# A state space stage laid out anew: half height blocks, three real products for a complex one, sums on the matrix engine

## The chip, the cores and the metric

One core of a Trainium2 chip runs the whole program in one launch. The metric is the device time in microseconds (us), median of three runs. TensorE (PE) multiplies matrices and transposes through an identity; VectorE (DVE) and GpSimd (POOL) do elementwise work; ScalarE (ACT) does activations and copies; SyncE (SP) issues most DMAs. Products accumulate in PSUM, which the other engines read.

## The reference, cut to what matters

Two model blocks on 256 tokens of width 2048: a diagonal state space mixer, two feed forward layers and an attention, then two layers that mix retention, attention and a recurrence. The change concerns the first stage alone:

```python
def s5_mixer(u, a_re, a_im, log_dt, b_re, b_im, c_re, c_im, d_skip, w_glu):
    lam_re, lam_im, dt = jnp.minimum(a_re, -1e-4), a_im, jnp.exp(log_dt)[:, None]
    mag, ang = jnp.exp(lam_re * dt), lam_im * dt
    lb_re, lb_im = mag * jnp.cos(ang), mag * jnp.sin(ang)          # lambda, [128 groups, 64 states]
    den = lam_re * lam_re + lam_im * lam_im
    nr, ni = lb_re - 1.0, lb_im
    coef_re = (nr * lam_re + ni * lam_im) / den
    coef_im = (ni * lam_re - nr * lam_im) / den
    bb_re = coef_re[..., None] * br - coef_im[..., None] * bi      # B bar, [g, p, 16]
    bb_im = coef_re[..., None] * bi + coef_im[..., None] * br
    ...                        # per group: s_t = lambda s_(t-1) + B bar u_t, from zero
    y = einsum('blgp,ghp->blgh', st_re, cr) - einsum('blgp,ghp->blgh', st_im, ci)
    g = jax.nn.gelu(y + d_skip * u)
    val, gate = jnp.split(g @ w_glu, 2, axis=-1)                   # the gated unit
    return val * jax.nn.sigmoid(gate)
```

Here u is the normed input in 128 groups of 16 channels; each group has 64 complex states.

## The kernel before, in words

`s5` (lines 257 to 743) does all up to the gelu; `glu` multiplies by `w_glu`. Tokens stand in 64 chunks of 4, groups are g = 64 gh + g'. V holds B bar times powers of lambda (a chunk's tokens into the state), W holds C times powers of lambda (state into the tokens), kd the blocks C lambda^d B within a chunk.

- Parameters: one group per partition. `exp_col`, sines and powers run on VectorE, squares of x for the norm on ScalarE. `regroup` orders x by group into M; `u_turn` transposes 64 blocks of 64x128; `u_scale` multiplies by the norm's scale on VectorE into U.
- `v_build` makes 8 blocks of 128x1024 by `cmul` (two products and a sum), 5 on VectorE and 3 on GpSimd. `w_build` makes 6 (3 and 3), `b_build` 2 on GpSimd.
- `turn` transposes four 128x128 blocks into a PSUM tile `psm`; `scatter` writes each tile by four ScalarE copies of 64x256 into `pad`, [128, gh, g', re/im, 64], where the rows of the other gh are zeros. GpSimd zeroes one quarter at the start and a DMA copies it to the other.
- `v_apply`: V x U for the states' inputs, over all 128 rows, in both column halves; ScalarE copies into S, [128, chunk, re/im, g'].
- kd: B bar x W in four column tiles (`psm<-pad,M`), four times: a ScalarE copy to `kd`, a GpSimd add of D, four DMAs to `kp` in DRAM and four back into M (lines 643 and 646).
- The scan (`step`, lines 651 to 673) on VectorE: four operations of 128x64 for each of 64 chunks, in two halves of the groups, the second 18 chunks behind.
- `own` adds U x M for all eight pairs of k-tiles, then `states` adds S x W; gelu on ScalarE, transposed and split in hi and lo (`split`), then the products of `glu`.

Every engine handle is wrapped by `InOrder`: ScalarE and GpSimd keep the order of the code from the start, VectorE and TensorE from the bar at line 396 on. All instructions of the stage carry line 230, that of the wrapper, so the profile tells them apart by their tiles. Tile x is also the store of the raw B and C. Behind the stage a steady loop of three products per weight tile runs (lines 65 to 67): load `wraw`, cast `whi` on ScalarE, subtraction `wlo` on VectorE.

Of the kernel before, what the change touches and what calls it, by code (L numbers as in the profile page):

```python
# [18 lines left out]
D = 2048  # L19
# [9 lines left out]
def load_unit(k, W, r0, nk, c0, cw):  # L29
    """k-tiles r0/128.. of W, split in two float32r parts whose sum is the float32 weight."""  # L30
# [83 lines left out]
def split_transposed(k, src, dst, kts, gain=None):  # L114
    """src(t, i): [128 tokens, 128] AP; dst hi/lo [128, k-tile, 256]; kts: k-tiles to fill."""
# [95 lines left out]
class InOrder:  # L211
    """an engine; after bar() instructions stay behind the last one, with strict each behind the one before"""
# [24 lines left out]
def exp_col(k, pool, x):  # L237
    """exp of [128, 1] to float32 rounding: 2**n times a polynomial of the rest"""
    nc = k.nc
    n = pool.tile([128, 1], F32, name="ec_n")  # L240
    p = pool.tile([128, 1], F32, name="ec_p")
    ni = pool.tile([128, 1], I32, name="ec_i")
# [14 lines left out]
def s5(k):  # L257
    """gelu of the state space mixer's output, transposed: hi/lo [128, k-tile, 256].

    Groups g = 64 gh + g'. Tokens go in 64 chunks of 4. The state times lambda, before each chunk:  # L260
    G' = lambda**4 G + sum_j lambda**(4-j) B u_j; y_l = C lambda**l G + sum_(j<=l) C lambda**(l-j) B u_j.
    """
# [36 lines left out]
    nc.sync.dma_start(dt, I["ssm_log_dt"][0].rearrange("(g o) -> g o", o=1))  # L299
    nc.sync.dma_start(ai, I["ssm_a_im"][0])  # L300
    nc.sync.dma_start(ar, I["ssm_a_re"][0])
    nc.sync.dma_start(gain, I["mix_norm"][0].rearrange("(g h) -> g h", h=16))
    for j in range(4):
        nc.sync.dma_start(xs[:, j, :], xr[:, j, :])
    for r, n in enumerate(("re", "im")):
        nc.sync.dma_start(braw[:, r], I["ssm_b_" + n][0])
    nc.sync.dma_start(pad[0:64, 1], pad[64:128, 0])
    nc.sync.dma_start(dsk, I["ssm_d"][0].rearrange("(g h) -> g h", h=16))
    for r, n in enumerate(("re", "im")):
        nc.sync.dma_start(craw[:, r], I["ssm_c_" + n][0])  # L310
# [3 lines left out]
    M = sU.tile([128, 2, 64, 64], F32, name="M")  # L314
    mflat = M.rearrange("p a b c -> p (a b c)")
    xn = mflat[0:64].rearrange("p (g a j h) -> p g a j h", a=2, j=4, h=16)
    junk = U[0:64].rearrange("p a b -> p (a b)")

    def regroup(j):
        o, i = xn[:, :, :, j, :], xs[:, j, :].rearrange("p (a g h) -> p g a h", a=2, h=16)  # L320
        if j == 3:
            nc.scalar.copy(o, i)
            return
        if j == 1:
            nc.gpsimd.tensor_copy(o, i)
            return
        nc.vector.bar()
        nc.vector.tensor_copy(o, i)
        nc.vector.bar()

    def square(j):
        nc.scalar.activation(junk[:, 0:D], xs[:, j, :], AF.Square, accum_out=ss[:, j:j + 1])

    regroup(1)
    for r in range(2):
        nc.gpsimd.tensor_tensor(
            braw[:, r], braw[:, r], gain.unsqueeze(1).to_broadcast([128, 64, 16]), ALU.mult
        )

    # parameters, groups on the partitions; pw[:, i] = lambda ** (4 - i)  # L340
    dtv = exp_col(ko, sB, dt)
    lr, th, sn, cs, em, nr, den, w0, tq, ang, cre = (
        sB.tile([128, 64], F32, name="p_" + n)
        for n in ("lr", "th", "sn", "cs", "em", "nr", "den", "w0", "tq", "ang", "cre")
    )
    mag, cim = th, ang
    nc.vector.tensor_scalar(lr, ar, -1e-4, None, ALU.min)
    cmul(den, tq, lr, lr, ai, ai, 1)
    nc.vector.reciprocal(den, den)
    nc.vector.tensor_scalar(th, lr, dtv, 0.5, ALU.mult, ALU.mult)  # L350
    nc.scalar.activation(th, th, AF.Tanh)
    nc.vector.tensor_scalar(ang, ai, dtv, None, ALU.mult)
    reduce_angle(ko, sB, ang, 64, wide=False)
    regroup(0)
    nc.vector.tensor_scalar(w0, ang, 0.5, None, ALU.mult)
    sincos(ko, sB, ang, 64, sn, cs)
    nc.scalar.activation(w0, w0, AF.Sin)
    nc.vector.tensor_scalar(em, th, -1.0, 1.0, ALU.mult, ALU.add)
# [3 lines left out]
    square(0)  # L362
    square(1)
    regroup(3)
    square(2)
    square(3)
# [9 lines left out]
    regroup(2)  # L376
# [8 lines left out]
    pc = sB.tile([128, 2, 4, 64], F32, name="pc")  # L385
    vpool = sB.tile([128, 2, 16, 64], F32, name="bb")
    t4 = vpool[:, 0, 0:4]
# [4 lines left out]
    cmul(pc[:, 0], t4, pw[:, :, 0], b1(cre), pw[:, :, 1], b1(cim), -1)  # L392
    cmul(pc[:, 1], t4, pw[:, :, 0], b1(cim), pw[:, :, 1], b1(cre), 1)
# [4 lines left out]
    def u_turn(g0, pool, nm):  # L398
        pt = pool.tile([128, 8, 64], F32, name=nm)
        for i in range(8):  # L400
            nc.tensor.transpose(pt[:, i, :], xn[:, g0 + i].rearrange("p a c d -> p (a c d)"), ident[:64, :64])
        return pt

    upt = [u_turn(8 * i, *((k.psg, "psg") if i < 4 else (k.psm, "psm"))) for i in range(6)]
    R = sA.tile([128, 64], F32, name="R")

    def rstd():
        rs = sA.tile([64, 4], F32, name="rs")
        nc.scalar.activation(rs, ss, AF.Sqrt, scale=1.0 / D, bias=k.eps[:64])
        nc.vector.reciprocal(rs, rs)  # L410
        rx = sA.tile([64, 2, 4, 16], F32, name="rx")
        nc.vector.tensor_copy(rx, rs.unsqueeze(1).unsqueeze(3).to_broadcast([64, 2, 4, 16]))
        pt = k.psm.tile([128, 64], F32, name="psm")
        nc.tensor.matmul(pt, rx.rearrange("p a c d -> p (a c d)"), ident[:64, :64], start=True, stop=True)
        nc.scalar.copy(R, pt)

    def u_scale(i):
        nc.vector.tensor_tensor(
            U[:, 8 * i:8 * i + 8, :], upt[i], R.unsqueeze(1).to_broadcast([128, 8, 64]), ALU.mult
        )  # L420
# [20 lines left out]

    def v_build(ri, b, on_pool=False, between=None):
        p0 = 16 * b
        if on_pool:
            eng = nc.gpsimd
# [112 lines left out]
    for i in range(4):  # L558
        u_scale(i)
# [921 lines left out]
```

## Time and profile before

| | |
|---|---|
| median of 3 runs | 3307.14 us (3305.91 to 3307.64) |
| profiled execution, span | 3304.2 us |
| PE, DVE, ACT, POOL busy | 97%, 59%, 49%, 3% of the span |
| instructions PE, DVE, ACT, POOL | 16691, 2983, 2151, 51 |
| TensorE's share of the chain that ended last | 90% |

The span is that of one profiled execution and 2.9 us below the median. In the chain of waits each piece is a start, a length, and the engine with the tile that it wrote. In timelines x counts the instructions of one row; a float32 product leaves two records on PE. The granted clock (PEclk) is the share of TensorE's full rate, 1.00 being 2.4 GHz and 0.5 being 1.2 GHz.

### The profile page before, as it was taken

The page shows a single profiled execution, that of the slowest core. Times are in us where ns is not written, and L with a number is a line of the kernel's source. Part 1 is how long each engine was busy: PE and PEld are TensorE (multiplying, and loading weights), DVE is VectorE, ACT ScalarE, POOL GpSimd, SP SyncE. Part 2 cuts the span into 40 slices and gives each one's busy share as a digit, 9 for nine tenths or more (in the row PEclk, how much of TensorE's full clock was granted, in tenths as well). Part 3 has the DMA queues.
Part 4 walks back from the last instruction along what each step waited for, and adds up shares of the span by engine and source line. Part 5 has one row for each costly group of instructions (what it writes and reads, how often), then busy time and mean ns, then how long its engine had stood idle before and what let it go on. Part 6 is the DMA issues. An engine that isn't in the chain of part 4 may idle for free.

```text
span 3304.2 us, 41770 instructions
## 1 busy us (share of the span) xinstructions
PE 3198.2 (97%) x16691; PEld 2721.6 (82%) x16702; DVE 1949.6 (59%) x2983; ACT 1618.6 (49%) x2151; POOL 97.6 (3%) x51
## 2 busy tenths in 40 slices
PE   3699999999999999999999999999999999999998
PEld 3488888888888888888888888888889988899887
DVE  9955544545554556666586454455457556676564
ACT  6634544344344555555554434444456455564463
POOL 7400000000000000000000000000000000000000
PEclk8799999999999999999999999999999999999999
DMA  3136565555555554555555555555565646556554
GB/s 90 35 93 193 177 203 187 192 192 185 193 192 196 170 189 161 171 176 163 181 167 185 187 192 189 191 191 195 187 186 164 202 151 204 166 164 196 158 193 166
DMA packets 333988, 575.93 MB, mean 174 GB/s; under 512 B 45793, under 2 KB 97505, under 8 KB 332897
## 3 DMA queue, kind: packets, MB, share of 16 engines
q1 hardware_dynamic: 300992, 565.04, 52.8%
q10 hardware_dynamic: 32800, 8.21, 1.2%
q8 instruction: 131, 2.15, 0.3%
q14 instruction: 65, 0.52, 0.0%
HBM read 568.50 MB, written 2.62 MB: 173 GB/s over the span
## 4 chain that ended last, share of the span: by engine, by line
PE 90%; DVE 6%; ACT 2%; DMA 1%; issue 0%; another core or an unknown queue 0%; ACTq 0%; SPq 0%; DVEq 0%
PE psg L65 28%; PE psg L67 28%; PE psg L66 28%; PE psm L123 1%; DVE S L230 1%; DVE sc L230 1%; DVE s5t L230 1%; PE psm L864 1%; DVE M L230 1%; DVE vb L230 1%; ACT whi L42 0%; PE psm L1198 0%; PE psm L801 0%; DMA wraw<-in_w_in 0%
## 5 line engine op out<-in xcount | busy, mean ns | idle before, releaser
L43 DVE TENSOR_TENSOR wlo<-wraw,whi 128x1024 fp32r<-128x1024 f32 (+1 forms) x1104 | 1295.6, 1178 | 1221.7 <-ACT whi L42 1220.2
L42 ACT CAST whi<-wraw 128x1024 fp32r<-128x1024 f32 (+1 forms) x1104 | 1116.7, 1017 | 1478.9 <-PE psg L67 1213.5
L65 PE MATMUL psg<-whi,act_hi 128*128 128x512 f32 (+1 forms) x4320 | 1651.5, 382 | 3.6 <-DVE act_lo L230 3.2
L67 PE MATMUL psg<-whi,act_lo 128*128 128x512 f32 (+1 forms) x4320 | 1642.8, 380 | 0.2
L66 PE MATMUL psg<-wlo,act_hi 128*128 128x512 f32 (+1 forms) x4320 | 1642.3, 380 | 0.0
L65 PEld LDWEIGHTS psg<-whi,act_hi 128*128 128x128 f32 x4320 | 811.8, 188 | 143.1 <-issue 4.9
L67 PEld LDWEIGHTS psg<-whi,act_lo 128*128 128x128 f32 x4320 | 811.2, 188 | 141.7 <-DVE act_lo L133 1.6
L66 PEld LDWEIGHTS psg<-wlo,act_hi 128*128 128x128 f32 x4320 | 811.8, 188 | 136.7
L230 ACT COPY pad<-psm 64x256 f32<-64x256 f32 x128 | 76.4, 597 | 4.3 <-PE psm L230 1.7
L230 DVE TENSOR_TENSOR S<-S,sc 128x64 f32<-128x64 f32 x248 | 48.7, 243 | 1.2
L230 DVE TENSOR_TENSOR sc<-A,S 128x64 f32<-128x64 f32 x248 | 44.1, 236 | 1.2
L133 DVE SCALAR_TENSOR_TENSOR act_lo<-psm,gain,act_hi 128x256 fp32r<-128x256 f32 x96 | 40.5, 478 | 5.1 <-ACT act_hi L132 4.6
L1155 ACT ACTIVATE in<-psg,rstd 128x384 f32<-128x384 f32 (+1 forms) x64 | 37.0, 606 | 10.3 <-PE psg L67 9.9
L128 DVE TENSOR_TENSOR act_lo<-psm,act_hi 128x512 fp32r<-128x512 f32 x60 | 38.3, 683 | 4.8 <-ACT act_hi L127 4.8
L65 PE MATMUL psg<-whi,attT_hi 128*128 128x512 f32 x96 | 38.9, 405 | 0.0
L132 ACT ACTIVATE act_hi<-psm,gain 128x256 fp32r<-128x256 f32 x96 | 38.9, 502 | 0.0
L194 ACT ACTIVATE sil<-psg,rstd 128x512 f32<-128x512 f32 x44 | 29.8, 690 | 17.9 <-PE psg L67 17.7
L67 PE MATMUL psg<-whi,attT_lo 128*128 128x512 f32 x96 | 37.5, 391 | 0.0
L66 PE MATMUL psg<-wlo,attT_hi 128*128 128x512 f32 x96 | 37.4, 390 | 0.0
L127 ACT CAST act_hi<-psm 128x512 fp32r<-128x512 f32 x60 | 32.0, 591 | 3.8 <-PE psm L123 3.8
L784 DVE SCALAR_TENSOR_TENSOR junk<-kk 128x128 f32<-128x128 f32 x128 | 28.8, 289 | 5.4 <-ACT kk L781 5.4
L207 DVE TENSOR_TENSOR x<-x,psg 128x512 f32<-128x512 f32 x48 | 30.9, 682 | 1.0 <-PE psg L67 1.0
(320 smaller groups left out, 1662.7 us busy)
## 6 DMA issues: line engine op xcount, KB each, us to landing
wraw<-in_w_gate_up SPq DMA_DIRECT2D x176, 1024.0 KB, 5.0
wraw<-in_w_down SPq DMA_DIRECT2D x88, 1024.0 KB, 5.1
wraw<-in_w_in SPq DMA_DIRECT2D x96, 768.0 KB, 4.6
wraw<-in_w_q SPq DMA_DIRECT2D x48, 1024.0 KB, 5.1
wraw<-in_w_glu SPq DMA_DIRECT2D x32, 1024.0 KB, 5.5
wraw<-in_w_kv SPq DMA_DIRECT2D x32, 1024.0 KB, 5.5
wraw<-in_w_in SPq DMA_DIRECT2D x32, 1024.0 KB, 5.0
wraw<-in_w_out SPq DMA_DIRECT2D x32, 1024.0 KB, 5.1
```

The costliest lines, as they stand in the source:

```text
L42: k.act_at = nc.scalar.copy(hi[:, :n, :cw], raw[:, a:a + n, :cw]).ins
L43: k.dve_at = nc.vector.tensor_tensor(lo[:, :n, :cw], raw[:, a:a + n, :cw], hi[:, :n, :cw].bitcast(F32), ALU.subtract).ins
L65: nc.tensor.matmul(o, a, wh, start=n == 0, stop=False)
L66: nc.tensor.matmul(o, a, wl, start=False, stop=False)
L67: k.mm = nc.tensor.matmul(o, b, wh, start=False, stop=n == total - 1).ins
L123: nc.tensor.transpose(pt[:, i, t * 128:(t + 1) * 128], src(t, i0 + i), k.ident)
L128: nc.vector.tensor_tensor(l, pt[:, :n, :], h.bitcast(F32), ALU.subtract)
L132: nc.scalar.activation(hi[:, kt, :], pt[:, i, :], AF.Copy, scale=gcol)
L133: nc.vector.scalar_tensor_tensor(lo[:, kt, :], pt[:, i, :], gcol, hi[:, kt, :].bitcast(F32), ALU.mult, ALU.subtract)
L230: done = fn(*args, **kw)
L864: nc.tensor.matmul(ps[:, 128:384], qT[g][:, h, 128:256], kT[:, h, :], start=True, stop=True)
L1155: nc.scalar.activation(dst[:, t, c:c + cw], ps[t][:, :cw], func, scale=rstd[:, t:t + 1])
```

## The change

- No `pad`. V and later W stand in one tile `VW`, [128, g', re/im, 64], where group half gh has the row half gh: products take 64 rows. A tile of four transposes is written by two ScalarE copies of 128x256.
- The parameters are loaded with a group g' and one half of the states on each partition, the two gh side by side, in 22 DMAs beside the four of x, in place of 9 and the one of the padded tile. The raw C comes in eight of them.
- The norm's scale is applied by four ScalarE activations before the transposes; U is copied by ScalarE.
- V: 23 VectorE operations of 128x1024 by the three product form (a sum of B's parts, and products with sums of the coefficient's parts). W and B bar: only three products each on VectorE; `turn` sums them in PSUM by float32 products with the identity and a negated one.
- S is [128, re/im, pair of groups, chunk, 2].
- `kd` has four buffers in place of two. The first loads of the gated unit's weights are issued ahead of the kp transfers.
- GpSimd keeps memsets and the adds of D.

```diff
-    pad = sA.tile([128, 2, 64, 2, 64], F32, name="pad")
-    nc.gpsimd.memset(pad[64:128, 0], 0.0)
...
+    VW = sA.tile([128, 64, 2, 64], F32, name="VW")
+    xn = VW[0:64].rearrange("c g a (j h) -> c g a j h", j=4)
+    for j in range(4):
+        nc.scalar.activation(
+            xn[:, :, :, j, :], xs[:, j, :].rearrange("c (a g h) -> c g a h", a=2, h=16), AF.Copy, scale=rs[:, j:j + 1]
+        )
...
     def turn(src):
...
-            nc.tensor.transpose(pt[:, i, :], src(i), ident)
+            parts = src(i)
+            if len(parts) == 1 and parts[0][1] > 0:
+                nc.tensor.transpose(pt[:, i, :], parts[0][0], ident)
+                continue
+            for n, (blk, sign) in enumerate(parts):
+                nc.tensor.matmul(
+                    pt[:, i, :], blk, ident if sign > 0 else nident, start=n == 0, stop=n == len(parts) - 1
+                )
...
+        nc.vector.tensor_tensor(sq(a), bs, over_h(pc[:, 0, j]), ALU.mult)
+        nc.vector.tensor_tensor(sq(b), braw[:, 1], over_h(ps_[:, j]), ALU.mult)
+        nc.vector.tensor_tensor(vre[:, :, :, j], sa(a), sa(b), ALU.subtract)
...
+                nc.scalar.copy(
+                    VW[:, :, ri, p0:p0 + 4], pt[:, :, 64 * half:64 * half + 64].rearrange("p i g -> p g i")
+                )
...
-                    ps[i // 8][64 * gh:64 * gh + 64, i % 8, :], pad[:, gh, g0 + i, ri, :], U[:, g0 + i, :],
-                    start=True, stop=True,
+                    ps[i // 8][rows, i % 8, :], VW[rows, g0 + i, ri, :], U[rows, g0 + i, :], start=True, stop=True
...
+    def w_build(l):
...
+        nc.vector.tensor_tensor(wk(f[0]), cs_, over(p2[:, i, 0]), ALU.mult)
+        nc.vector.tensor_tensor(wk(f[1]), cw[:, 0], over(p2d[:, i - 1]), ALU.mult)
+        nc.vector.tensor_tensor(wk(f[2]), cw[:, 1], over(p2s[:, i - 1]), ALU.mult)
...
+    def b_turn(ri):
...
+                        for n, (w, one) in enumerate(pick):
+                            nc.tensor.matmul(
+                                pt[o0:o0 + 32, h, :], f[w][rows, a, :, h0 + h], one[rows, rows],
+                                start=n == 0, stop=n == 1, tile_position=(64 * half, o0),
+                            )
...
-        G, N = S[:, c, :, gs], S[:, c + 1, :, gs]
+        G, N = (S[:, :, gs, i, :] for i in (c, c + 1))
...
-                            ys[kb][rows, i, :], S[:, :, r, g], pad[:, gh, g, r, :], start=False, stop=False
+                            ys[kb][rows, i, :], S[rows, r, g // 2, :, g % 2], VW[rows, g, r, :], start=False, stop=False
```

The order changes in three places. First VectorE, from the last build of W to the first step of the scan, in the kernel before (M is the store of W, pw the powers, s5t the second product, S and sc the scan's):

```order
L230 TENSOR_TENSOR M<-x,pw 128x1024
L230 TENSOR_TENSOR s5t<-x,pw 128x1024
L230 TENSOR_TENSOR M<-M,s5t 128x1024 [waits DVE_49]
L230 TENSOR_TENSOR s5d<-s5d,s5gain 128x16 [waits DMAHW3_49]
L230 TENSOR_TENSOR sc_0_1345<-A_267,S 128x64 [waits Activation_49]
L230 TENSOR_TENSOR sc_0_1346<-A_268,S 128x64
L230 TENSOR_TENSOR S<-S,sc_0_1345 128x2x32 [waits DMAHW7_49,DMAHW5_49,DVE_49]
L230 TENSOR_TENSOR S<-S,sc_0_1346 128x2x32 [waits DVE_49]
```

Here the last build is two products and their sum, and the scan waits for ScalarE's copies and for loads.

VectorE at the same place after the change (wk are the products of B and W, pcd, pcs, p2d and p2s differences and sums of the coefficients and powers):

```order
L230 TENSOR_TENSOR wk<-bs,pc 128x1024 [waits DVE_49,PE_49]
L230 TENSOR_TENSOR wk<-x,pcd 128x1024 [waits PE_49]
L230 TENSOR_TENSOR wk<-x,pcs 128x1024 [waits PE_49]
L230 TENSOR_TENSOR wk<-cs__319,pw_308 128x1024 [waits DVE_49,PE_49]
L230 TENSOR_TENSOR wk<-x,p2d 128x1024 [waits PE_49]
L230 TENSOR_TENSOR wk<-x,p2s 128x1024 [waits PE_49]
L230 TENSOR_TENSOR s5d<-s5d,s5g_87 128x16 [waits DMAHW1_49,DMAHW0_49]
L230 TENSOR_TENSOR sc_0_1569<-A_356,S 128x64 [waits Activation_49]
L230 TENSOR_TENSOR sc_0_1570<-A_357,S 128x64
L230 TENSOR_TENSOR S<-S,sc_0_1569 128x2x16x2 [waits DVE_49]
```

Three products stand in place of two and a sum; they and those of B now wait for TensorE, which reads the buffers they take.

Second ScalarE, from the copies of dT (the D part) through those of kd to the first gelu, before (the numbers of DMAHW are DMA queues):

```order
L230 COPY dT<-psm 16x32 [waits PE_49,Pool_49]
L230 COPY dT<-psm 16x32 x3
L230 COPY kd<-psm 128x512 [waits PE_49] x2
L230 COPY kd<-psm 128x512 [waits DMAHW1_49,DMAHW2_49,DMAHW0_49,DMAHW3_49,PE_49,Pool_49]
L230 COPY kd<-psm 128x512 [waits DMAHW3_49,DMAHW4_49,DMAHW2_49,DMAHW5_49,PE_49,Pool_49]
L230 ACT_TABLE_LOAD [waits DMAHW4_49,DMAHW5_49,DMAHW3_49,DMAHW6_49,PE_49]
L230 ACTIVATE kd<-psg 128x512 [waits Pool_49]
```

The third and fourth copy of kd wait for the transfers that read the first two.

ScalarE at the same place after (wraw and whi are raw and cast weights of the gated unit):

```order
L230 COPY dT<-psm 16x32 [waits PE_49,Pool_49]
L230 COPY dT<-psm 16x32 x3
L230 COPY kd<-psm 128x512 [waits PE_49]
L42 CAST whi<-wraw 128x1024 [waits DMAHW3_49,DMAHW2_49,DMAHW4_49,DMAHW1_49,DMAHW5_49,DMAHW0_49,DVE_49]
L42 CAST whi<-wraw 128x1024
L230 COPY kd<-psm 128x512 [waits PE_49]
L42 CAST whi<-wraw 128x1024 [waits DMAHW5_49]
L42 CAST whi<-wraw 128x1024
L230 COPY kd<-psm 128x512 [waits PE_49] x2
L230 ACT_TABLE_LOAD [waits DMAHW1_49,DMAHW6_49,DMAHW0_49,DMAHW7_49,PE_49]
```

Four casts of the gated unit's weights have moved in between the copies, and no copy of kd waits for the transfers of an earlier one.

Third TensorE where W begins, before (x is the raw C, M the built W, psg the products of V and U):

```order
L230 MATMUL psm<-ident,x 128x128 x3
L230 MATMUL psg<-U,pad 64x64 x32
L230 MATMUL psm<-ident,M 128x128 [waits DVE_49,PE_49,Activation_49]
L230 MATMUL psm<-ident,M 128x128 x3
L230 MATMUL psm<-ident,M 128x128 [waits PE_49,Activation_49]
L230 MATMUL psm<-ident,M 128x128 x3
L230 MATMUL psg<-U,pad 64x64 x32
```

Eight transposes of W stand between two parts of V's products.

TensorE where W begins after the change (x again the raw C, nident the negated identity):

```order
L230 MATMUL psg<-U,VW 64x64 x15
L230 MATMUL psm<-ident,x 128x128 [waits DMAHW2_49,DMAHW3_49,DMAHW1_49,DMAHW0_49]
L230 MATMUL psm<-ident,x 128x128 x7
L230 MATMUL psm<-nident,x 128x128 [waits DMAHW6_49,DMAHW7_49,DMAHW5_49,DMAHW4_49]
L230 MATMUL psm<-nident,x 128x128 x7
L230 MATMUL psm<-ident,wk 128x128 [waits DVE_49,PE_49,Activation_49]
L230 MATMUL psm<-nident,wk 128x128 [waits DVE_49]
L230 MATMUL psm<-ident,wk 128x128
```

All of V's products have moved ahead of W, and each block of W is a pair of products, one of them here with the negated identity.

## Rows read from the trace of the kernel before

**Rows 1.** Windows: us, busy us of PE, PEld, DVE, ACT, POOL; PEclk, DMA share, GB/s

```profile
28.00:70.00 42.00, 19.35 (x98) 15.97 (x98) 41.83 (x27) 31.97 (x59) 36.23 (x13) 0.79 0.06 22
...
101.00:139.00 38.00, 15.49 (x149) 10.37 (x153) 36.77 (x195) 36.30 (x65) 13.06 (x13) 0.53 0.08 28
...
226.00:246.00 20.00, 20.00 (x89) 16.54 (x88) 9.10 (x8) 9.89 (x12) 0.00 (x0) 1.00 0.48 154
```

**Rows 2.** The chain of waits in order of time: start, us, what

```profile
28.00 0.43 DVE pc L230
...
108.86 0.36 DVE sc L230 x2
...
158.49 0.28 DVE S L230 x2
...
165.18 3.05 DMA M<-kp
...
173.68 9.54 PE psg L230 x128
...
217.55 3.32 ACTq L145
...
222.31 0.47 PE psg L65
```

**Rows 3.** Timeline, all engines, first 30 us: start, us, engine, operation

```profile
1.00 6.93 POOL L230 MEMSET pad<- 64x8192 f32 x1
...
2.80 0.15 DVE L230 TENSOR_SCALAR dt<-dt 128x1 f32<-128x1 f32 x1 [1.90 <-DMA dt<-in_ssm_log_dt]
...
4.05 3.92 DVE L230 TENSOR_SCALAR ec_p<-ec_p,dt 128x1 f32<-128x1 f32 x1
...
13.23 1.21 DVE L230 COPY M<-S 64x2048 f32<-64x2048 f32 x1
...
16.20 1.89 ACT L230 ACTIVATE U<-S 64x2048 f32<-64x2048 f32 x1
...
16.78 2.37 DVE L230 TENSOR_TENSOR pw<-pw,t 128x64 f32<-128x64 f32 x1
...
24.46 3.65 PE L230 MATMUL psg<-ident,M 64*128 64x64 f32 x32 [24.46 <-DVE M L230]
```

**Rows 4.** The same, VectorE's builds of V without and with GpSimd beside

```profile
56.31 1.21 DVE L230 TENSOR_TENSOR vb<-x,pc 128x1024 f32<-128x1024 f32 x1
...
64.88 3.76 DVE L230 TENSOR_TENSOR vb<-vb,s5t 128x1024 f32<-128x1024 f32 x1
```

**Rows 5.** Groups by line: busy us, mean ns of one, idle before

```profile
L230 ACT COPY pad<-psm 64x256 f32<-64x256 f32 x128 | 76.4, 597 | 4.3 <-PE psm L230 1.7
...
L230 ACT COPY S<-psg 128x504 f32<-128x504 f32 x16 | 8.9, 581 | 4.0 <-PE psg L230 3.9
...
L230 ACT COPY M<-psm 64x256 f32<-64x256 f32 x16 | 5.9, 368 | 0.2
```

**Rows 6.** Timeline of TensorE's products: V, kd, own, then attention's

```profile
97.08 2.08 PE L230 MATMUL psg<-U,pad 128*64 128x64 f32 x64
...
140.82 2.00 PE L230 MATMUL psm<-pad,M 128*16 128x64 f32 x128
...
161.44 1.15 PE L230 MATMUL psg<-M,U 64*64 64x64 f32 x32
...
1285.23 0.38 PE L899 MATMUL psm<-pT,vv 128*128 128x128 f32 x2
1285.45 0.39 PE L900 MATMUL psm<-pT,vv 128*128 128x128 f32 x2
```

**Rows 7.** Timeline of ScalarE's last copies of W into the padded tile

```profile
108.34 29.40 ACT L230 COPY pad<-psm 64x256 f32<-64x256 f32 x48
```

**Rows 8.** Timeline of SyncE's first kp transfers, at their issue

```profile
141.76 4.09 SPq L643 DMA_DIRECT2D kp<-kd  x6
```

**Rows 9.** The page's DMA issues: KB each, us to landing

```profile
wraw<-in_w_glu SPq DMA_DIRECT2D x32, 1024.0 KB, 5.5
```

More of the change, by code (lines that the diff above doesn't have):

```diff
@@ L331, in square @@
[L331 to L342, printed above, removed]
+    nident = sB.tile([128, 128], F32, name="nident")
+    dtv = exp_cols(ko, sB, dt, 2).unsqueeze(2).to_broadcast([128, 2, 32])
@@ L396, in s5 @@
         e.strict = True
[L398 to L419, printed above, removed]
-        )
+    VW = sA.tile([128, 64, 2, 64], F32, name="VW")
+    xn = VW[0:64].rearrange("c g a (j h) -> c g a j h", j=4)
+    for j in range(4):
+        nc.scalar.activation(
+            xn[:, :, :, j, :], xs[:, j, :].rearrange("c (a g h) -> c g a h", a=2, h=16), AF.Copy, scale=rs[:, j:j + 1]
+        )
+    for i in range(8):
+        pt = k.psg.tile([128, 8, 64], F32, name="psg")
+        for g in range(8):
+            nc.tensor.transpose(pt[:, g, :], xn[:, 8 * i + g].rearrange("c a j h -> c (a j h)"), ident[:64, :64])
+        nc.scalar.copy(U[:, 8 * i:8 * i + 8, :], pt)
+    p2 = sB.tile([128, 4, 2, 2, 2, 32], F32, name="pw2")
+    for to in range(2):
+        for half in range(2):
+            for r in range(2):
+                nc.scalar.copy(
+                    p2[64 * to:64 * to + 64, :, r, :, half, :],
+                    pw[64 * half:64 * half + 64, :, r].rearrange("p i (a q) -> p i a q", a=2),
+                )
+    p2 = p2.rearrange("p i r a x q -> p i r (a x q)")
     def turn(src):
@@ L465, in v_turn @@
-    def v_turn(ri, b):
-        vf = built[ri, b]
-        for i0 in (0, 4):
-            scatter(turn(lambda i: vf[:, i0 + i, :]), into_pad(ri, 16 * b + 2 * i0))
-    S = sA.tile([128, 64, 2, 64], F32, name="S")
-    def v_apply(ri, pair):
-        g0 = 16 * pair
+            parts = src(i)
[5 more added lines that the diff above has]
+                    pt[:, i, :], blk, ident if sign > 0 else nident, start=n == 0, stop=n == len(parts) - 1
+                )
@@ new lines, in s5 @@
+    gb = gain.unsqueeze(2).to_broadcast([128, 2, 32, 16])
+    for r in range(2):
+        bv = braw[:, r].rearrange("p (a q) h -> p a q h", a=2)
+        nc.vector.tensor_tensor(bv, bv, gb, ALU.mult)
+    nc.vector.tensor_tensor(bs, braw[:, 0], braw[:, 1], ALU.add)
+    k1 = []
+    for j in range(4):
+        a, b = work(), work()
+        k1.append(a)
+        nc.vector.tensor_tensor(sq(a), bs, over_h(pc[:, 0, j]), ALU.mult)
+        nc.vector.tensor_tensor(sq(b), braw[:, 1], over_h(ps_[:, j]), ALU.mult)
+        nc.vector.tensor_tensor(vre[:, :, :, j], sa(a), sa(b), ALU.subtract)
@@ new lines, in s5, with v_turn @@
+    for j in range(4):
+        b = work()
+        nc.vector.tensor_tensor(sq(b), braw[:, 0], over_h(pd[:, j]), ALU.mult)
+        nc.vector.tensor_tensor(vim[:, :, :, j], sa(k1[j]), sa(b), ALU.add)
+    def v_turn(ri, v):
+        v = v.rearrange("p q a j h -> p q (a j h)")
+        for q0 in range(0, 32, 4):
+            pt = turn(lambda i: [(v[:, q0 + i], 1)])
+            for half in range(2):
+                p0 = 32 * half + q0
+                nc.scalar.copy(
+                    VW[:, :, ri, p0:p0 + 4], pt[:, :, 64 * half:64 * half + 64].rearrange("p i g -> p g i")
+                )
@@ L482, in v_apply @@
             g = g0 + 8 * i
-            nc.scalar.copy(S[:, 1:64, ri, g:g + 8], ps[i][:, :, 0:63].rearrange("p g c -> p c g"))
-    A1 = sA.tile([128, 2, 64], F32, name="A1")
-    A2 = sA.tile([128, 2, 64], F32, name="A2")
-    def a_turn():
-        pt = k.psm.tile([128, 128], F32, name="psm")
-        nc.tensor.transpose(pt, pw[:, 0].rearrange("p r q -> p (r q)"), ident)
-        for gh in range(2):
-            rows = slice(64 * gh, 64 * gh + 64)
-            for r in range(2):
-                nc.scalar.copy(A1[rows, r], pt[0:64, rows])
-                nc.scalar.activation(A2[rows, r], pt[64:128, rows], AF.Copy, scale=1.0 if r else -1.0)
@@ L536, in b_turn @@
-    def b_turn(ri):
-        bf = built["bb"][:, ri].rearrange("p (a b) q -> p a (b q)", b=2)
-        for i0 in (0, 4):
-            scatter(
-                turn(lambda i: bf[:, i0 + i, :]),
-                lambda rows, gh, half: bT[rows, ri, 2 * i0 + half:2 * i0 + 8:2, :],
-            )
-    def u_late(g0):
-        upt.append(u_turn(g0, k.psm, "psm"))
-    v_build(0, 3, True)
-    v_build(1, 3, True)
-    v_build(0, 0, between=rstd)
-    u_late(48)
-    u_scale(4)
-    u_scale(5)
-    v_turn(0, 0)
@@ L578, in s5 @@
-    for ri, l in ((1, 2), (0, 3), (1, 3)):
-        w_build(ri, l, True)
-    for pair in range(2):
-        for ri in range(2):
-            v_apply(ri, pair)
-    v_apply(0, 2)
+            nc.scalar.copy(
+                S[:, ri, g // 2:g // 2 + 4, 1:64, :], ps[i][:, :, 0:63].rearrange("p (g e) c -> p g c e", e=2)
+            )
+    A1 = sA.tile([128, 2, 32, 2], F32, name="A1")
+    A2 = sA.tile([128, 2, 32, 2], F32, name="A2")
+    def a_turn():
+        pt = k.psm.tile([128, 2, 32, 2], F32, name="psm")
+        for r in range(2):
+            nc.tensor.transpose(pt[:, r].rearrange("p g e -> p (g e)"), p2[0:64, 0, r, :], ident[:64, :64])
+        for r in range(2):
+            nc.scalar.copy(A1[:, r], pt[:, 0])
+            nc.scalar.activation(A2[:, r], pt[:, 1], AF.Copy, scale=1.0 if r else -1.0)
@@ new lines, in s5, with wk, over @@
+    p2s, p2d = (sB.tile([128, 3, 128], F32, name=n) for n in ("p2s", "p2d"))
+    built = {}
+    cw = craw.rearrange("p r h a q -> p r h (a q)")
+    def w_build(l):
+        def wk(t):
+            return t.rearrange("p (h q) -> p h q", h=8)
+        def over(a):
+            return a.unsqueeze(1).to_broadcast([128, 8, 128])
+        i = 4 - l
+        f = [work(), work(), work()]
+        nc.vector.tensor_tensor(wk(f[0]), cs_, over(p2[:, i, 0]), ALU.mult)
+        nc.vector.tensor_tensor(wk(f[1]), cw[:, 0], over(p2d[:, i - 1]), ALU.mult)
+        nc.vector.tensor_tensor(wk(f[2]), cw[:, 1], over(p2s[:, i - 1]), ALU.mult)
+        built[l] = [wk(t) for t in f]
@@ new lines, in w_turn @@
+    def w_turn(l):
+        for ri in range(2):
+            for h0 in (0, 4):
+                if l == 0:
+                    pt = turn(lambda i: [(cw[:, ri, h0 + i], 1 - 2 * ri)])
+                else:
+                    f = built[l]
+                    pick = ((0, 1), (2, -1)) if ri == 0 else ((0, -1), (1, -1))
+                    pt = turn(lambda i: [(f[n][:, h0 + i], sign) for n, sign in pick])
+                for half in range(2):
+                    c0 = 16 * l + 8 * half + h0
+                    nc.scalar.copy(
+                        VW[:, :, ri, c0:c0 + 4], pt[:, :, 64 * half:64 * half + 64].rearrange("p i g -> p g i")
+                    )
@@ new lines, in s5, with b_build @@
+    bT = sA.tile([128, 2, 16, 64], F32, name="bT")
+    def b_build():
+        f = built["b"] = [work(), work(), work()]
+        nc.vector.tensor_tensor(sq(f[0]), bs, over_h(cre), ALU.mult)
+        nc.vector.tensor_tensor(sq(f[1]), braw[:, 0], over_h(pd[:, 4]), ALU.mult)
+        nc.vector.tensor_tensor(sq(f[2]), braw[:, 1], over_h(ps_[:, 4]), ALU.mult)
+    def b_turn(ri):
+        f = [t.rearrange("p (a q h) -> p a q h", a=2, h=16) for t in built["b"]]
+        pick = ((0, ident), (2, nident)) if ri == 0 else ((0, ident), (1, ident))
+        for h0 in (0, 8):
+            pt = k.psm.tile([128, 8, 64], F32, name="psm")
+            for h in range(8):
+                for a in range(2):
+                    for half in range(2):
+                        rows = slice(64 * half, 64 * half + 64)
+                        o0 = 64 * a + 32 * half
+                        for n, (w, one) in enumerate(pick):
+                            nc.tensor.matmul(
+                                pt[o0:o0 + 32, h, :], f[w][rows, a, :, h0 + h], one[rows, rows],
+                                start=n == 0, stop=n == 1, tile_position=(64 * half, o0),
+                            )
+            nc.scalar.copy(bT[:, ri, h0:h0 + 8, :], pt)
@@ new lines, in s5 @@
+    v_turn(0, vre)
+    for part in range(4):
+        v_apply(0, part)
+    a_turn()
+    v_turn(1, vim)
+    for part in range(4):
+        v_apply(1, part)
+    nc.gpsimd.memset(S[:, :, :, 0, :], 0.0)
+    nc.vector.tensor_tensor(cs_, cw[:, 0], cw[:, 1], ALU.add)
+    nc.vector.tensor_tensor(p2s, p2[:, 1:4, 0], p2[:, 1:4, 1], ALU.add)
+    nc.vector.tensor_tensor(p2d, p2[:, 1:4, 1], p2[:, 1:4, 0], ALU.subtract)
+    w_turn(0)
+    for l in (1, 2):
+        w_build(l)
+        w_turn(l)
+    b_build()
@@ L607, in s5 @@
     k.act = [k.ctx.enter_context(tc.tile_pool(name="acta", bufs=1))]
-    nc.gpsimd.memset(M[:, 0], 0.0)
+    M = sU.tile([128, 64, 64], F32, name="M")
+    nc.gpsimd.memset(M, 0.0)
     zb = sA.tile([128, 512], BF16, name="zb")
```

258 lines of the change are left out of this document (93 added, 165 removed).

## The prediction

> **What bounds the kernel now.** I read the windows by stage first [rows 1]. From 226 us on TensorE is busy 20.00 of 20 us, and it stays so: nothing of the change lies there, and the order of instructions behind the stage is untouched, so what the state space stage gains or loses passes to the end one to one. From 28 to 70 us VectorE is the full engine (41.83 of 42), with GpSimd at 36.23 beside it; from 101 to 139 it is ScalarE (36.30 of 38), with TensorE at a granted clock of 0.53.
>
> Then the chain of waits [rows 2]. It is VectorE until the parameters are there (28.43), through the builds, and through the scan behind them, whose second round begins at 108.86 and whose last sum ends at 158.77. Then come the transfers of the blocks (the last M lands at 165.18 + 3.05 = 168.23), the chunk's own outputs, the states' outputs from 173.68, and a DMA issue that holds ScalarE from 217.55. The first product of the gated unit starts at 222.31. That start is what I forecast.
>
> Last come timelines of engines, the groups by line and the DMA issues, for prices [rows 3 to 9].
>
> **The way to the last build.** *Parameters.* The 64x8192 memset of the padded tile runs on GpSimd from 1.00 to 7.93, and a 128x1 VectorE operation beside it took 3.92 us, where one before took 0.15 [rows 3]: 3.7 us go. A regroup copy of 1.21 goes too. Three more issues stand ahead of the last parameter, +1.3 at the pitch of that queue (estimated at 0.43 each). The sines' inputs were there at 14.8 and will be at 12.4 with a few shorter steps. Four squares (1.89 plus an accumulator read of 0.19 each) end at 20.8, table load and root at 22.5. The parameters' products ended at 28.43; the sines 2.4 earlier, a second regroup copy gone, a multiply that took 2.37 beside GpSimd back at some 0.25, give the same 22.5.
>
> *Inputs.* The norm's scale is now four ScalarE activations of 64x2048 at 1.9: 30.3. Then 64 transposes of 64x64 at 3.65/32 = 0.114: 37.6, and the last copy +0.6. Eight small copies of the powers end at 41.2. ScalarE is the limit: VectorE's fifteen builds (2 + 1 + 12) at 1.13 to 1.21 [rows 4] end at 39.6, hidden by a margin of only 1.6. A build beside GpSimd took 3.76, so it is VectorE without GpSimd that makes this possible.
>
> *Scatter.* 128 copies of 64x256 into the padded tile at 597 ns become 64 of 128x256. Copies of before into M, with short contiguous runs, took 368; the new ones write four adjacent words, so I take 0.37, with 0.597 as upper end [rows 5]. One part of V, 16 copies, is 5.9 us (at most 9.6). The new copies read the accumulator across rows; the S copy did that already, 581 ns for 504 elements, per element no dearer than the M copy (1.15 against 1.44 ns).
>
> The Trainium skill (SBUF — State Buffer, Door 1: The DMA port swizzle, note on cachelines) says that SBUF access pays for each new 16-byte line unless a line is hit at least twice, and that accumulator access that is not contiguous slows matmuls. With its first half 597 against 368 agrees; for copies the S copy doesn't bear out the second. Read for copies as well, it would put V's two parts at 9.6 each and the time 7 us later.
>
> *V's products.* They were full height with zeros, and are half height now, gh on the two row halves. The nearest row is own's: 16 products (32 records; a float32 product leaves two) in 1.15 us, 0.072 each [rows 6], near the 0.065 of V's full height products (64 records in 2.08). V's 128 products of one part: 9.2. Copies 41.2 to 47.1, products to 56.2, late copies and the turn of lambda +1.4, then 5.9 and 9.1: 72.6.
>
> *Sums on TensorE.* First W block: 8 transposes and 8 products with the negated identity, 2.6. The others: 3 x 32 products of 128 columns at 0.22, start to start [rows 6] = 21.1. B: 256 products of 64 rows and 32 columns at own's 0.072 = 18.4. Its ends are 0.031 (B times C of before, four column tiles, 64 products in 2.00) and 0.15 (the states of before): 8 to 38. Sum 42.1: 114.7. ScalarE's 36 copies and VectorE's builds lie beside it. VectorE's last build waits until TensorE has read the third W block, whose buffers it takes: 89.3, so the scan begins at 92.9. Queued behind that wait are the D product and the scan alone.
>
> **From the last build to the gated unit.** Last copy to first kp issue took 141.76 - 137.74 = 4.0, issue to last M 26.5 [rows 2, 7, 8]: 118.7 and 145.2. Four kd buffers in place of two don't shorten this, as each M transfer waits for its kp to land. Own takes 5.3 as before: T = 150.5. The scan without GpSimd is 158.77 - 108.86 + 0.8 for its first round = 50.7: it ends at 143.6, under T by 7.
>
> Two loads of the gated unit's weights now stand ahead of the first kp on SyncE, and four casts on ScalarE between copies of kd. A load lands in 5.5 us [rows 9] and one kd feeds 6.6 us of transfers, so I take nothing; uncovered it is 6.
>
> States: 256 products took 4 x 9.54 = 38.2 [rows 2]. S was read at a stride of 512 bytes; now it is 8, at half height, as own's: 4 x 4.6 = 18.4. From 173.68 to 222.31 is 48.6; less 19.8 is 28.8. ScalarE's DMA issue (3.5) no longer stands ahead of the first products: their weights are split by then, and two units, 11 us at the steady 222 ns a product, cover it: 25.2.
>
> The first product thus starts at 150.5 + 25.2 + 0.5 for copies that wait = 176.2, 46.1 earlier than 222.3. The span was 3304.2, the median is 2.9 above it: 3258.1 + 2.9 = **3261 us**. Of the 46, 23 come before kp, 20 in the states, 3 in the issue. Late next are the transfers of kp and M, with the scan 7 behind.
>
> **Rivals.** *The scan is dearer.* Its operands are pairs of words 512 bytes apart, where they were runs of 32 words. If each element pays as in the padded copy ((597 - 368)/256 = 0.9 ns, on 64 elements), an operation goes from 0.135 to 0.19, the scan to 71 and T to 164; at 0.24, T is 182. Time 3274 to 3292, middle 3281. For: no row shows VectorE on such pairs. Against: a pair is two words, not one.
>
> *Strided weights keep the old price.* If the states stay at 0.15, +20: 3281; if B, whose weights jump by 64 bytes, costs it too: 3301. For: the only rows of strided weights are the states. Against: those were full height.
>
> *Half height products run one at a time.* A product of 64 columns alone is half of one of 128, 0.107; V, B and states, 768 x 0.035 = 27 us: 3288. Against: own's 0.072, on two row halves and one bank, is already under 0.107.
> The Trainium skill (TensorEngine Tiling (Array Packing), Restrictions and Gotchas, Gotcha 1: PSUM Pressure) says that different row tiles can't access the same accumulator bank at once. By that rule this rival would be right; own's row contradicts it.
>
> *Half of W and B at the low clock*, as the 0.53 of 101 to 139 suggests, though the new work is denser: 42/2 = 21, 3282.
>
> *Slower than before.* TensorE stays at the lower of its levels (1.2 in place of 2.4 GHz) until the states are done: W and B +42, the first kd +2, states +18, 62 lost against 46 won: 3323. It decides from 46 lost on. For: 0.53 in just this work. Against: products at 97.08 and 161.44 ran at the full rate as soon as they were dense.
>
> **How the numbers follow.** The forecast has 0.61, with its own range of 3250 (B at its low end) to 3274 (loads +6, copies +7). Dear scan 0.13, strided weights 0.10, one at a time 0.03, half low clock 0.06, slower 0.03, more gain than forecast 0.04. A measurement of this kernel can tell 0.2%, 6.6 us: under 3300.5 is faster. Strided weights at their upper end fall on that line, 0.02 for the same. Faster 0.95, same 0.02, slower 0.03. The range, 3244 to 3294, leaves out the rivals' upper ends and the largest gains.
>
> **What would show it.** First kp issue at 119, last M at 145; V's last product at 73; VW copies at 370 ns; no VectorE build over 1.3 us; B's products at 0.07; scan operations at 0.135, the last at 144; states 4.6 us for 128 records; first product of the gated unit at 176. It is wrong if the scan ends after own, if the granted clock from 73 to 115 lies near 0.5, or if something behind the stage moves.

## The result, and the profile after

The changed kernel takes 3270.22 us (3268.73 to 3270.99, 4 runs) against 3306.52 of the kernel before on the same chip: ratio 0.9889, 95% interval 0.9875 to 0.9903. The forecast was 3261, in a range of 3244 to 3294. The gain is 36.3, the forecast's 46.1. Profiled, the span is 3268.9.

First the windows after (columns as in [rows 1]):

```profile
50.00:80.00 30.00, 28.44 (x564) 27.88 (x560) 11.70 (x12) 18.25 (x51) 3.98 (x2) 1.00 0.01 3
80.00:105.00 25.00, 20.38 (x615) 19.77 (x614) 20.20 (x102) 6.72 (x18) 0.00 (x0) 1.00 0.24 87
105.00:125.00 20.00, 15.24 (x529) 12.40 (x532) 20.00 (x136) 7.20 (x14) 3.48 (x7) 0.71 0.48 143
125.00:155.00 30.00, 22.88 (x372) 15.95 (x374) 29.69 (x212) 0.27 (x1) 0.57 (x1) 0.85 0.21 41
...
195.00:215.00 20.00, 20.00 (x90) 16.57 (x89) 9.20 (x8) 9.63 (x10) 0.00 (x0) 1.00 0.60 202
```

TensorE is nearly full from 50 to 80, at a granted clock of 1.00 where [rows 1] had 0.53 and 0.79. Then VectorE is: 20.00 of 20 and 29.69 of 30. The steady loop, 20.00 of 20, is as before.

The chain of waits after (start, us, what; compare [rows 2]):

```profile
68.06 16.90 PE psm L230 x150
84.98 0.26 DVE wk L230
85.23 0.88 issue
86.12 1.22 DVE wk L230
87.42 0.27 DVE sc L230 x2
...
164.90 0.36 DVE sc L230 x2
...
170.53 0.55 DVE act_lo L230
...
185.77 0.47 PE psg L65
```

TensorE holds VectorE's last build until 84.98, as forecast (89.3 there); from 87.42 on the chain is the scan, to 165.7. Kp, M and own, the bound of the forecast, aren't on it.

Groups by line after (busy us, mean ns; the VW copies answer to [rows 5], the builds to [rows 4]):

```profile
L230 ACT COPY VW<-psm 128x256 f32<-128x256 f32 x64 | 19.8, 414 | 16.1 <-PE psm L230 15.8
...
L230 DVE TENSOR_TENSOR vre<-wk 128x1024 f32<-128x1024 f32 x4 | 4.9, 1225 | 0.1
```

Timeline of VectorE and TensorE after, the two ends of the scan and what waits:

```profile
151.32 5.45 PE L230 MATMUL psg<-VW,S 64*64 64x64 f32 x128 [5.90 <-DVE S L230]
...
157.23 4.06 PE L230 MATMUL psg<-VW,S 64*64 64x64 f32 x128
...
165.71 4.06 PE L230 MATMUL psm<-VW,S 64*64 64x64 f32 x128 [2.13 <-DVE S L230]
```

```profile
165.18 0.48 DVE L230 TENSOR_TENSOR S<-S,sc 128x64 f32<-128x64 f32 x2
165.90 4.63 DVE L43 TENSOR_TENSOR wlo<-wraw,whi 128x1024 fp32r<-128x1024 f32 x4 [0.24 <-issue]
170.45 0.62 DVE L230 TENSOR_TENSOR act_lo<-psg,act_hi 128x256 fp32r<-128x256 f32 x1
```

TensorE waits for the scan twice, and the splits stand behind the scan's end and behind four subtractions for the gated unit. The same engine in the kernel before, at the end of its scan:

```profile
171.40 0.64 DVE L230 TENSOR_TENSOR S<-S,sc 128x64 f32<-128x64 f32 x4
172.06 0.36 DVE L230 TENSOR_TENSOR sc<-A,S 128x64 f32<-128x64 f32 x2
...
185.84 0.48 DVE L230 TENSOR_TENSOR S<-S,sc 128x64 f32<-128x64 f32 x2
```

There the scan ended at 186.3, not at 158.77. At 158.77 the chain of [rows 2] left it for a transfer, while the scan went on beside it. Its first round, in the same chain of waits, stood beside GpSimd:

```profile
101.66 2.43 DVE sc L230 x2
104.08 2.32 DVE S L230
106.42 2.41 DVE S L230
```

So it took 84.7 us, 6.4 more than in the changed kernel, and those 6.4 lie in this round (7.2 in place of 0.8). In both kernels it is 80 rounds: 18 of one half of the groups at some 0.79, 44 of both at some 1.08, 18 of the other half; that is 76 us, and some rounds took longer.

### The profile page after: what moved, and what is told of

Read it like the earlier page. It is cut to its first block, busy times and chain, and to the rows that moved or that the text cites. A ratio compares the mean times of both kernels' runs of the same rounds, so it can differ in the third digit from the quotient of the medians.

```text
span 3268.9 us, 42975 instructions
## 1 busy us (share of the span) xinstructions
PE 3190.0 (98%) x17338; PEld 2720.7 (83%) x17349; DVE 1899.5 (58%) x2988; ACT 1567.4 (48%) x2088; POOL 12.8 (0%) x23
## 4 chain that ended last, share of the span: by engine, by line
PE 92%; DVE 5%; ACT 2%; DMA 1%; issue 0%; SPq 0%; another core or an unknown queue 0%; DVEq 0%; ACTq 0%
PE psg L67 29%; PE psg L65 29%; PE psg L66 29%; DVE S L230 1%; DVE sc L230 1%; PE psm L123 1%; PE psm L230 1%; PE psm L855 1%; DMA wraw<-in_w_in 1%; DVE wlo L43 1%; PE psg L230 1%; PE psm L1189 0%; PE psm L792 0%; ACT act_hi L132 0%; ACT whi L42 0%
## 5 line engine op out<-in xcount | busy, mean ns | idle before, releaser
L230 PE MATMUL psg<-ident,VW 64*128 64x64 f32 x64 | 7.1, 311 | 29.8 <-ACT VW L230 29.8
L230 PEld LDWEIGHTS psg<-ident,VW 64*128 64x128 f32 x64 | 6.9, 220 | 29.8 <-issue 29.8
```

Of the source, the lines that this page charges most:

```text
L230: done = fn(*args, **kw)
```

## The experiments

Theory A: the scan, 78 us long, bounds the changed kernel. B: the loss against the forecast lies in the tail behind the scan. A second question was which parts brought the gain. "First product" is the gated unit's first that follows the last wait, 222.31 before and 185.77 after.

| run | median us | ratio to before, 95% | first product |
|---|---|---|---|
| changed | 3270.22 | 0.9889 (0.9875 to 0.9903) | 185.77 |
| early_scan | 3256.78 | 0.9849 (0.9836 to 0.9863) | 170.23 |
| lead2 | 3265.20 | 0.9876 (0.9862 to 0.9889) | 180.99 |
| wlo_late | 3266.23 | 0.9879 (0.9863 to 0.9894) | 182.07 |
| copy_order | 3277.07 | 0.9911 (0.9898 to 0.9925) | 192.56 |
| pool_beside | 3285.36 | 0.9938 (0.9925 to 0.9952) | 202.09 |
| early_old_s | 3269.15 | 0.9886 (0.9873 to 0.9900) | 183.41 |
| best | 3251.56 | 0.9834 (0.9821 to 0.9847) | 165.96 |
| before_dve | 3309.90 | 1.0011 (1.0002 to 1.0020) | 226.31 |
| before_runs | 3303.73 | 0.9988 (0.9980 to 0.9997) | 220.46 |
| before_dve_runs | 3288.85 | 0.9943 (0.9929 to 0.9956) | 205.52 |

**early_scan**

```diff
-        f = [work(), work(), work()]
+        f = [vflat[:, 3072:4096], mflat[:, 0:1024], mflat[:, 1024:2048]] if l == 3 else [work(), work(), work()]
...
-        f = built["b"] = [work(), work(), work()]
+        f = built["b"] = [vflat[:, 1024 * i:1024 * i + 1024] for i in range(3)]
```

> The changed kernel, with the products of B bar and of the last W block written into the storage of V's two built halves, which TensorE has read by 59 us, instead of into the six shared buffers. Nothing else moves. Theory A (the scan sets the end of the stage: in the changed kernel it runs from 87.3 to 165.7, 78 us, not the 50.7 of the forecast, and splits stand behind it on VectorE): VectorE's builds end near 65, the scan starts when the last state input is copied, 68.7, and ends near 147; own's end (145) becomes the bound, the first product of the gated unit starts near 170 in place of 185.8, and the time is 16 us less than the changed kernel's, near 3254. Theory B (the loss against the forecast lies behind the scan, in ScalarE's and VectorE's alternating casts and gelus): the tail keeps its length whatever the scan does and the time falls by less than 4 us.

A holds: the first product came 15.5 earlier, at 170.23, and the time is 13.4 less, where 16 were expected. The scan began at 65.1 and not at 68.7, since its first half needs only half of the groups; it took the same 78.3. Its two ends, on VectorE:

```profile
65.10 0.35 DVE L230 TENSOR_TENSOR sc<-A,S 128x64 f32<-128x64 f32 x2
...
142.90 0.48 DVE L230 TENSOR_TENSOR S<-S,sc 128x64 f32<-128x64 f32 x2
```

TensorE is now late itself. Its timeline:

```profile
108.22 0.39 PE L230 MATMUL psm<-zb 128*128 128x512 bf16 x1 [4.04 <-POOL zb L230]
...
144.96 1.15 PE L230 MATMUL psm<-M,U 64*64 64x64 f32 x32
145.94 4.01 PE L230 MATMUL psg<-VW,S 64*64 64x64 f32 x128
...
170.23 0.47 PE L65 MATMUL psg<-whi,act_hi 128*128 128x512 f32 x1 [0.95 <-DVE act_lo L230]
```

States follow own with no wait for the scan. The 4.04 is the edit's own cost: M is cleared on GpSimd only after its storage has served the last W block, and the zero tile of the bank products is cleared behind it.

**lead2**: `lead = 18` becomes `lead = 2`.

> The changed kernel with the second half of the scan 2 chunks behind the first instead of 18. Alone, a step of one half takes 0.79 us (four operations that wait for each other), two halves together 1.08. Theory A: the scan is 64 rounds, about 4 x 0.79 + 60 x 1.08 = 68 us instead of 78, its end moves from 165.7 to 155.5, the first half's end from 151.3 to 153.8; then TensorE's states outputs, dense from 153.8 to 172, and the splits bind, and the time falls by 4 to 9 us, to 3261 to 3266. Theory B: no change beyond 2 us, or a loss of 2.4 from the later first half.

**wlo_late**: the first four `wlo` subtractions are issued after the fourth split.

> The changed kernel with VectorE's four subtractions for the gated unit's first weights (4.6 us, from 165.9 to 170.5, between the scan and the first split) behind the first four splits instead. Theory A: the splits of the first four k-tiles start 4.6 us earlier; what is behind them waits for gelus on ScalarE, so some of the 4.6 comes back: the time falls by 2 to 4.6 us, to 3266 to 3268. Rival: the first products need these weights anyway and wait for them: within 1 us of the changed kernel.

In the traces the first product moves by 4.8 (lead2, where the scan ends at 156.7) and 3.7 (wlo_late), within what A gave; the intervals of the two times overlap that of the changed kernel, so the times alone don't show it.

**copy_order**

```diff
-                    VW[:, :, ri, p0:p0 + 4], pt[:, :, 64 * half:64 * half + 64].rearrange("p i g -> p g i")
+                    VW[:, :, ri, p0:p0 + 4].rearrange("p g i -> p i g"), pt[:, :, 64 * half:64 * half + 64]
```

> The changed kernel with the same 64 copies of 128x256 out of the transposes' accumulators, but each written in the order of the source (64 groups for one word, then the next word: a step of 512 bytes for each element, as into the padded tile of before) instead of four adjacent words at a time. Theory (the pattern of the write sets the price: 597 ns then, 0.29 from start to start now): a copy takes about 0.6, V's two parts of 16 copies 9.6 each in place of 4.6, so V's last input to the scan comes 10 us later, and so do the W products behind it, the scan and the end: 3280. Rival (what saved was the number of copies, 64 in place of 128): copies stay near 0.3, the time within 2 us of 3270.

ScalarE's timeline of the second part of V, first the changed kernel, then this one:

```profile
55.76 4.57 ACT L230 COPY VW<-psm 128x256 f32<-128x256 f32 x16
```

```profile
58.68 7.19 ACT L230 COPY VW<-psm 128x256 f32<-128x256 f32 x16
```

The order of the write sets the price, 4.57 against 7.19 for the same 16 copies; 0.45 a copy, not 0.6, so the loss was 7 and not 10.

**pool_beside**: eight `nc.gpsimd.tensor_tensor` of 128x1024 into a tile of their own.

> The changed kernel with eight products of 128x1024 added on GpSimd beside VectorE's builds of V; nothing reads their result. Theory (a VectorE build beside GpSimd takes over 3 us, as rows of the kernel before show): from 25.6 on, for some 24 to 27 us, builds go at about the pace of GpSimd's, 3.3 each, so the real half of V is there near 56 instead of 39.8 and everything behind it 16 us later: 3286. Rival (the two engines only looked slow together because of the access patterns of that kernel): builds stay at 1.22 and the time within 2 us of 3270.

VectorE's timeline there; GpSimd's products begin at 25.66:

```profile
25.61 1.23 DVE L230 TENSOR_TENSOR wk<-bs,pc 128x1024 f32<-128x1024 f32 x1
26.75 2.92 DVE L230 TENSOR_TENSOR wk<-x,pcs 128x1024 f32<-128x1024 f32 x1
29.70 3.28 DVE L230 TENSOR_TENSOR vre<-wk 128x1024 f32<-128x1024 f32 x1
```

Builds went from 1.23 to 2.9 to 3.4, and the time up by 15: the price of GpSimd beside is shown.

**early_old_s**: S as [128, chunk, re/im, group] again, on top of early_scan.

> The kernel early_scan (3256.8) with the old layout of the scan's tile: chunk, re/im, group, so that the state weights of TensorE step by 512 bytes again while products stay half height; there the states' products (four groups of 64) bind TensorE from 145.9 on. If the stride made a state product cost 0.15 us, a group takes 9.6 us instead of 4.06, 22 us in all, of which some 20 are late at the gated unit: 3277. If half height on two row halves made it cheap, groups stay near 4.1 to 4.6 and the time near 3257. The scan operations, with runs of 32 words, are expected the same as with pairs either way: 0.135 us each in the two-half rounds.

TensorE's timeline there:

```profile
146.50 7.27 PE L230 MATMUL psg<-VW,S 64*64 64x64 f32 x128
...
154.25 7.33 PE L230 MATMUL psg<-VW,S 64*64 64x64 f32 x128
```

The time is 12.4 over early_scan, between the two. Neither alternative holds alone: of the 5.5 us that a group of states lost (9.54 in [rows 2], 4.06 now), the stride made 3.3, measured at half height, and the height 2.2, measured at 512 bytes. All these groups ran at a granted clock of 1.00. The scan's operations are unmoved: 217 ns busy with runs of 32 words, 217 to 221 with pairs.

**before_dve**: `nc.gpsimd` becomes `nc.vector` in the builds of the kernel before.

> The kernel before with one part of the change alone: the eight builds that ran on GpSimd (two of V, three of W, two of B, and their temporaries) run on VectorE in the same places of its order. Theory A (VectorE without GpSimd beside it takes 1.14 us per build operation, with it 3 to 3.8): 48 operations in 55 us end near 89 instead of 101, ScalarE's copies into the padded tile, 0.6 each, then bind and end near 125 instead of 138; first kp transfer and everything behind it 10 to 13 us earlier: 3294 to 3297. Rival: ScalarE's copies were the bound all along: under 3 us.

**before_runs**: its copies into the padded tile without the rearrangement of the target, the source rearranged instead.

> The kernel before with one part of the change alone: its 128 copies into the padded tile are written group by group, four words of a group (each second word) before the next group, in place of one word of all 64 groups. Copies fall from 0.6 to about 0.3 to 0.37, the last W copy from 137.7 to about 122 and the last M to about 153. Theory (the scan is hidden right behind the bound: builds beside GpSimd still end at 99.3, the scan starts at 101.7 as before and its first half ends at 172, where states started at 173.6 before): the time falls by 1 to 3 us only, to 3303 to 3305. Rival (ScalarE's copies alone bound the kernel before, since VectorE's builds alone did not help): 13 to 15 us, 3291 to 3293.

**before_dve_runs**: both.

> The kernel before with both parts: builds on VectorE alone and copies group by group; tile, products, scan layout and everything behind stay old. Theory (the two bounds stand one right behind the other, so that each alone gives nothing and both give much): builds end near 89, copies no longer hold them, the scan starts near 89 and its first half ends near 152, last M near 130 to 140; states, at the old 9.6 a group, run from 152 in place of 173.6: 19 to 22 us less, 3285 to 3287. The rest of the change's 36 us is then the states' price and the tail behind the scan. Rival: no more than the sum of the single effects, under 5 us.

Groups by line, and ScalarE's last copies of W (compare [rows 7]), of before_dve:

```profile
L230 ACT COPY pad<-psm 64x256 f32<-64x256 f32 x128 | 76.4, 597 | 4.3 <-PE psm L230 1.7
...
L230 DVE TENSOR_TENSOR s5t<-x,pc 128x1024 f32<-128x1024 f32 x5 | 6.1, 1215 | 0.0
```

```profile
113.39 29.41 ACT L230 COPY pad<-psm 64x256 f32<-64x256 f32 x48
```

The first states on TensorE in before_runs, behind the last own:

```profile
156.08 1.15 PE L230 MATMUL psm<-M,U 64*64 64x64 f32 x32
171.79 9.61 PE L230 MATMUL psg<-pad,S 128*64 128x64 f32 x128 [14.56 <-DVE S L230]
```

Groups by line of before_dve_runs, and the same place on TensorE:

```profile
L230 ACT COPY pad<-psm 64x256 f32<-64x256 f32 x128 | 48.4, 378 | 4.3 <-PE psm L230 1.7
...
L230 DVE TENSOR_TENSOR s5t<-x,pc 128x1024 f32<-128x1024 f32 x5 | 6.1, 1216 | 0.0
```

```profile
149.40 1.15 PE L230 MATMUL psm<-M,U 64*64 64x64 f32 x32
156.77 9.61 PE L230 MATMUL psg<-pad,S 128*64 128x64 f32 x128 [6.22 <-DVE S L230]
```

Builds alone: each costs 1.2, not 2.8, and the kernel is slower by 3 to 4, because the same 76.4 us of copies bind, begin 4.0 later (41.18, where it was 37.16) and end 5.1 later (142.8, where it was 137.7); theory A's 10 to 13 missed there. Copies alone: 4 less; in the trace the first product comes 1.9 earlier, as the scan then binds (states wait for it until 171.79, where they started at 173.61 before), and the rest of the 4 is not placed. Both: 19 less, where 19 to 22 were expected. Two bounds stood one right behind the other.

**best**

```diff
+        nc.vector.tensor_tensor(f[2], f[0], f[2], ALU.subtract)
+        nc.vector.scalar_tensor_tensor(f[1], f[0], -1.0, f[1], ALU.mult, ALU.subtract)
...
-    lead = 18
+    lead = 8
...
-    nc.gpsimd.memset(M, 0.0)
     zb = sA.tile([128, 512], BF16, name="zb")
     nc.gpsimd.memset(zb, 0.0)
+    nc.gpsimd.memset(M, 0.0)
```

> early_scan with three more edits: the sums of the three built W blocks on VectorE (two operations a block) and plain transposes on TensorE in place of pairs of identity products; the second half of the scan 8 chunks behind the first; the small zero tile of the bank products cleared on GpSimd before M and not behind it, which held the first block products for 4.0 us in early_scan. Theory A (what binds behind the scan's start is TensorE's way to the first kp transfer, and then the scan): VectorE's builds end near 72, kp starts near 97 instead of 113, the first half of the scan ends near 137 and the whole near 143, states start at 137 instead of 145.9, the first product of the gated unit near 161: 3248, 8 to 9 us under early_scan. Rival (sums on TensorE cost nothing there, as copies or the scan hide them): within 2 us of 3257.

5.2 less than early_scan where 8 to 9 were expected, with intervals that overlap a little; it beats both kernels. First kp issue 93.67, states' start 139.36 (behind the first half of the scan), first product 165.96: VectorE is the bound again. Which of its three edits brought how much was not tried.

## Why the prediction was right, and where it was wrong

| step | forecast | measured |
|---|---|---|
| root of the norm | 22.5 | 21.8 |
| V's copies, real part, end | 47.1 | 47.1 |
| V's products end | 72.6 | 68.1 |
| last build's wait ends | 89.3 | 85.0 |
| first kp issue | 118.7 | 110.7 |
| last own ends | 150.5 | 145.4 |
| scan ends | 143.6 | 165.7 |
| first product | 176.2 | 185.8 |

- **The step that failed** is "The scan without GpSimd is 158.77 - 108.86 + 0.8 for its first round = 50.7". It took a place where the chain leaves an engine for the end of the engine's work. The scan takes 78.3 (87.4 to 165.7), 28 more. With 78.3 in the forecast's own sum it would have ended at 171, 21 behind own, and been named as the bound. early_scan shows it: the scan moved alone brought 15.5. By the prediction's own sign, "It is wrong if the scan ends after own", its account of the bound was wrong: the scan ended at 165.7, own at 145.4.
- **The time was near by luck.** With the scan at 78.3 the same sum gives 3282. The scan's start came 5.5 earlier than forecast and what lies between the bound and the first product was 5.6 shorter, so the miss was 9 us and not 21.
- **The rival of the dearer scan** had the right place by the wrong mechanism: a pair costs what a run costs.
- **The way to kp** was right in kind and on the safe side: 8 us better. A part of V's products took 7.7, not 9.1, the copies of V's second part 4.6, not 5.9, and B's sums 13.9 (85.09 to 98.98), not 18.4. A built W block took 7.1, near the 7.0 forecast. That the copies of V's real part end at 47.1, as forecast, is luck: they took 6.0 because they waited for TensorE's transposes, not by their own price. From the first kp issue to the last own it was 34.7, not 31.8; whether the two loads ahead of the transfers cost these 3 us was not tried.
- **"It is VectorE without GpSimd that makes this possible"** was half of it. Builds alone brought nothing (before_dve); the copies, which the forecast priced but put beside the builds, were the other half (before_dve_runs).
- **Copies**: 0.37 was forecast; 16 take 4.57, 0.29 from start to start.
- **States**: 4 x 4.6 forecast, 4.06 measured in a group at the full clock. The first, behind a wait of 5.90, took 5.45, at a granted clock of 0.58 from 146.5 to 153.7. The forecast gave the gain to stride and height together; both have a part.
- **One at a time** did not come: V's 128 products of one part took 7.68, 0.060 each, under the 0.107 of one alone; that 0.107 is the prediction's estimate, half of a 128 column product, and no run took one alone. The Trainium skill (TensorEngine Tiling (Array Packing), Restrictions and Gotchas, Gotcha 1: PSUM Pressure) would have them one by one in a bank; the trace disagrees.
- **Low clock**: 0.71 and 0.85 came, from 105 to 155, but on kd's later products and around the wait behind own, while the scan ran beside them and was the bound. W and B ran at 1.00 (windows from 68 to 106).
- **The tail**: 25.2 was forecast behind own; 20.1 lie between the scan's end and the first product, 4.6 of it the four subtractions, which the forecast took as hidden. The DMA issue did fall off the chain.

The account of the 36.5 us by which the first product moved: the scan ends 20.7 earlier (it starts 14.2 earlier, and 6.4 lost beside GpSimd in its first round are gone), and the tail behind it is 15.9 shorter than the 36.0 of before, where the dear states lay. This is a sum between two points and not a list of causes: in the kernel before, the chain went through own and the states, not through the scan's end. Of the causes, the builds and copies together are shown at 19 us; that the other 17 are the states' price and the tail is argued. The stride's 12.4 was measured on early_scan, where the states bind, and not on the changed kernel.

## What to carry to other kernels

The end of a piece in a chain of waits is where the chain changed engines, not where that engine's work ended: read the length of a loop from the engine's own timeline, last row included. Before an engine is relieved, look which other engine would be full over the same stretch: two bounds one behind the other give little singly (here 3 to 4 us lost and 4 won, against 19 won together). A shared buffer pool can couple engines: here six work buffers let TensorE decide when VectorE's scan could start, and storage that lay idle was worth 13 us.

## What the runs showed of the hardware that was not expected

State weights read at a step of 512 bytes cost TensorE 7.3 us for 64 half height products, at 8 bytes 4.06. And a copy of ScalarE that writes word by word over 64 groups costs 0.45 where one that writes four adjacent words costs 0.29, from the same source.
